# Dilated attention of a hybrid decoder step: the transposes of p of two units in one place, directly behind the values of two others

## The chip, the core and the metric

The kernel runs on one core of a Trainium2 chip. The metric is the device time of one execution in microseconds (us), lower is better. Engines are named as in the profile: PE is TensorE (PEld its weight loads), DVE is VectorE, ACT is ScalarE, POOL is GpSimd, SP issues most DMAs.

## What is computed

One inference step of a one-layer decoder trunk: a Mamba-2 group, a dilated sliding-window attention group and a memory cross-attention group share one input projection and one output projection. The change touches the dilated attention of the prompt (1024 positions, 8 heads of 64). The reference, cut to it:

```python
DILATED_PAIRS = ((128, 1), (512, 4), (2048, 16))
def dilated_prompt(q, k, v):
    for window, dil in DILATED_PAIRS:
...
        sc = jnp.einsum('bnqrhe,bnkrhe->bnrhqk', qb, kb) * scale
        sc = jnp.where(valid[None, :, None, None], sc, -jnp.inf)
        m = jnp.max(sc, axis=-1)
        p = jnp.exp(sc - m[..., None])
        l = jnp.sum(p, axis=-1)
        acc = jnp.einsum('bnrhqk,bnkrhe->bnqrhe', p, vb)
...
        parts.append((back(m), back(l), acc))
    return combine_dilations(parts)
```

`combine_dilations` weighs the three accumulators by their maxima and denominators.

## The kernel before

The dilated attention is done in four passes, `window_attention(hp)` (line 779), one for each pair of heads. A pass begins with transposes of q and k (`qkT`, line 799) and then works through N = 24 units, each one block of 128 queries for both heads: eight of dilation 1, eight of dilation 4, eight of dilation 16. A unit has k = 1 or 2 key blocks of 128.

A unit goes through three stages, each a local function that is called with a step number n:

- `scores(n)` (line 834): four PE matmuls of unit n (`sc`, lines 842 and 843); then for each head DVE masks and takes the maximum (line 847) and ACT takes the exponential with its sum (line 849). The result is the SBUF tile `p`, of which there are 7 buffers.
- `transposed(n)` (line 853): 2k PE transposes of p of unit n-3 into one PSUM bank (`pT`, line 862), and one DVE copy of that bank to SBUF (`pt`, line 863).
- `values(n)` (line 867): only at even n, for the two units n-6 and n-5: the matmuls of pt with v (`o`, line 877; the trace has two records for each). Every fourth unit ends with an ACT copy of the bank (`acc`, line 890).

The order on PE is the order in which the program issues; the other engines' order is set by the scheduler. The step loop sets it:

```python
        for n in range(N + 5):
...
            for work in ((values, transposed), (scores,)):
                ns = sum(w(n) for w in work)
                if ns:
                    yield ns
```

After each yield `drive` (line 150) issues projection matmuls ("fill": tiles `z` and `ga`, lines 336 to 338, in threes) worth 0.6 of the yielded nanoseconds, and `spend` (line 111) moves background work on. The background work of a pass is the `merge` (line 905) of the pass before it. It transposes the maxima and denominators (`mlT`, line 909), goes through DRAM, and then issues eight weight-broadcast matmuls `wb` (line 946), each into a PSUM bank that a DVE product reads (`acc`, line 947). Between two of them lie 900 ns of issued work.

`bank(tag, name)` (line 52) hands out PSUM banks of a tag in turn. `psum_phase("B2", acc=2, sc=2, tp=2, o=2)` gives the tag `tp` two banks, and qkT, mlT, pT and wb all take theirs from it: a request gets the bank of the request before the last, and its writer waits until that one has been read.

Of the kernel before, what the change touches and what calls it, by code (L numbers as in the profile page):

```python
# [11 lines left out]
F32 = mybir.dt.float32  # L12
# [8 lines left out]
P = 128  # L21
# [15 lines left out]
def hybrid_step(ctx: ExitStack, tc: tile.TileContext, i, o):  # L37
# [14 lines left out]
    def bank(tag, name):  # L52
        return phase["pool"].tile([P, 512], F32, tag=tag, name=name, bufs=phase["bufs"][tag])
# [15 lines left out]
    def as32(ap):  # L69
        return ap.bitcast(F32)  # L70
# [21 lines left out]
    def open_pool(name, side="left"):  # L92
        guards[name] = tc.tile_pool(name=name, bufs=1, side=side, reuse_waits="tile")
        return guards[name].__enter__()
# [619 lines left out]
    for f in range(8):  # L714
# [4 lines left out]
        else:  # L719
            if f == 4:  # L720
                until("qc1")
            tp = bank("tp", f"mvT{f}")
# [19 lines left out]
    ap_ = open_pool("apool")  # L742
# [36 lines left out]
    def window_attention(hp):  # L779
# [9 lines left out]
        for c in range(2):  # L789
# [5 lines left out]
            for dst, src in ((q2[0], lambda b: qv[:, b, 0:P]), (kk[0], lambda b: kv[:, b, 0]), (q2[1], lambda b: qv[:, b, P:2 * P]),  # L795
                             (kk[1], lambda b: kv[:, b, 1]), (None, lambda b: lv[:, b])):
                tp = bank("tp", f"qkT_{hp}{c}")
# [24 lines left out]
        units = []  # L822
# [10 lines left out]
        ps, pts, ob, N = {}, {}, None, len(units)  # L833
        def scores(n):
            nonlocal ob
            if n < N:
                pair, u, q, qs_, ks_, vts = units[n]
                w = len(vts) * P
                mask = mask3 if pair == 2 else mask1[:, 256 - w:]
                sc = bank("sc", f"sc_{hp}{n}").rearrange("p (h k) -> p h k", h=2)  # L840
                for h in range(2):
                    PE.matmul(sc[:, h, :w], lhsT=qs_(q[h]), rhs=ks_(kk[h]), start=True, stop=False)  # L842
                    PE.matmul(sc[:, h, :w], lhsT=qs_(q[h]), rhs=ks_(kl[h]), start=False, stop=True)  # L843
                for h in range(2):
                    p = ps[n, h] = ap_.tile([P, 256], F32, tag="p", name=f"p_{hp}{n}{h}", bufs=7)
                    mx, den = ml[:, 0, h, pair, u:u + 1], ml[:, 1, h, pair, u:u + 1]
                    DVE.tensor_tensor_reduce(out=p[:, :w], in0=sc[:, h, :w], in1=mask, scale=-0.125, scalar=HUGE,  # L847
                                             op0=ALU.add, op1=ALU.min, accum_out=mx)
                    ACT.activation(p[:, :w], p[:, :w], AF.Exp, scale=-1.0, bias=mx, accum_out=den)  # L849
                return 4 * max(116.0, w / 2.4 + 12.0)  # L850
            return 0.0

        def transposed(n):
            nonlocal ob
            if 3 <= n < N + 3:
                k = len(units[n - 3][5])
                tp = bank("tp", f"pT_{hp}{n}").rearrange("p (h k) -> p h k", h=2)
                pt = pts[n - 3] = ap_.tile([P, 2, 256], F32, tag="pt", name=f"pt_{hp}{n}", bufs=3)
                for h in range(2):
                    p = ps.pop((n - 3, h))  # L860
                    for t in range(k):
                        PE.transpose(tp[:, h, t * P:(t + 1) * P], p[:, t * P:(t + 1) * P], ident)  # L862
                DVE.tensor_copy(pt[:, :, :k * P], tp[:, :, :k * P])  # L863
                return 218.0 * k
            return 0.0

        def values(n):

# [24 lines left out]
        for n in range(N + 5):  # L893
            if hp < 3 and n in (12, 14):
                load_qk(hp + 1, n // 2 - 6)
            if hp < 3 and n == 18:
                split_qk(hp + 1, 0)
# [5 lines that stand above are left out]
        later(0.0, merge(hp, ml, acc))  # L903

    def merge(hp, ml, acc):


        tp = bank("tp", f"mlT_{hp}")
        PE.transpose(tp[:96, :P], ml.rearrange("p a h r u -> p (a h r u)"), ident)
        mlT = ap_.tile([96, P], F32, tag="mlT", name=f"mlT_{hp}", bufs=1)  # L910
        DVE.tensor_copy(mlT, tp[:96, :P])
        SP.dma_start(ml_d[hp], mlT)
        rb = ap_.tile([16, 2, 3, P], F32, tag="rb", name=f"rb_{hp}", bufs=1)
        for a in range(2):
            src = ml_d[hp, a * 48:(a + 1) * 48].rearrange("(h r u) n -> r h (u n)", h=2, r=3)
            SP.dma_start(rb[:, a, 0], src[0].rearrange("h (t n) -> h t n", t=8))
            for h in range(2):
                SP.dma_start(rb[8 * h:8 * h + 8, a, 1], src[1, h].rearrange("(r t m) -> t r m", r=4, t=8))
                SP.dma_start(rb[8 * h:8 * h + 8, a, 2], src[2, h].rearrange("(r t m) -> t r m", r=8, t=8))
        mm = ap_.tile([16, P], F32, tag="mm", name=f"mm_{hp}", bufs=1)  # L920
        wt = ap_.tile([16, 3, P], F32, tag="wt", name=f"wt_{hp}", bufs=1)

        nat = lambda a, r: rb[:, a, r].rearrange("p (r m) -> p m r", r=(1, 4, 8)[r])
        as_ = lambda t, r: t.rearrange("p (m r) -> p m r", r=(1, 4, 8)[r])
        DVE.tensor_copy(mm, rb[:, 0, 0])
        for r in (1, 2):
            DVE.tensor_tensor(as_(mm, r), as_(mm, r), nat(0, r), op=ALU.min)
        for r in range(3):
            POOL.tensor_tensor(as_(wt[:, r], r), as_(mm, r), nat(0, r), op=ALU.subtract)
        ACT.activation(wt, wt, AF.Exp)  # L930
        for r in range(3):
            POOL.tensor_tensor(nat(1, r), as_(wt[:, r], r), nat(1, r), op=ALU.mult)
        DVE.tensor_copy(mm, rb[:, 1, 0])
        for r in (1, 2):
            POOL.tensor_tensor(as_(mm, r), as_(mm, r), nat(1, r), op=ALU.add)
        DVE.reciprocal(mm, mm)
        POOL.tensor_tensor(wt, wt, mm.unsqueeze(1).to_broadcast([16, 3, P]), op=ALU.mult)
        ACT.copy(wts[:16], wt)
        DVE.tensor_tensor(wts[32:48], wt, as32(wts[:16]), op=ALU.subtract)
        yield 18000.0  # L940
        flat_ = lambda t: t.rearrange("p k n -> p (k n)")
        aacc[hp] = ap_.tile([P, S], F32, tag="att", name=f"att_{hp}")
        out_ = aacc[hp].rearrange("p (t n) -> p t n", n=P)
        for T in range(8):
            wb = bank("tp", f"wb_{hp}{T}")[:, :3 * P]
            PE.matmul(wb, lhsT=selw[:, T], rhs=flat_(wts), start=True, stop=True)
            DVE.tensor_tensor(flat_(acc[:, T]), flat_(acc[:, T]), wb, op=ALU.mult)
            if T % 4 == 3:
                part = slice(T - 3, T + 1)
                POOL.tensor_tensor(acc[:, part, 0], acc[:, part, 0], acc[:, part, 1], op=ALU.add)  # L950
                POOL.tensor_tensor(out_[:, part], acc[:, part, 0], acc[:, part, 2], op=ALU.add)
            yield 900.0
        finished.add(f"att{hp}")
# [636 lines left out]
```

## Time and profile before

| | us |
|---|---|
| median of 3 runs (lowest to highest) | 1181.92 (1181.43 to 1184.21) |
| the profiled execution: its own time | 1178.0 |
| its span, first to last instruction | 1176.2 |
| PE busy | 1106.5 (94% of the span) |
| DVE, ACT, POOL busy | 714.1, 476.5, 395.8 |
| the four attention passes and their fill | about 380 to 638 us of the span |

In the timeline a row is one or more instructions of the same kind that follow each other on an engine. PE is pipelined, so that rows overlap; the cost of a matmul is the distance from its start to the start of the next one. A time in square brackets is idle time of the engine before the row and what ended it.

### The profile page before, as it was taken

What the parts mean: (1) busy time and instruction counts of PE and PEld (TensorE: products, weight loads), DVE (VectorE), ACT (ScalarE), POOL (GpSimd) and SP (SyncE); (2) the same over time, 40 slices, a digit from 0 to 9 for tenths busy, and PEclk for the clock granted to TensorE, in tenths of its full rate; (3) what the DMA queues carried; (4) which work ended last, traced back from release to release, by engine and by line L of the source; (5) the groups of instructions that cost most, each with busy time, mean ns of one, the idle gap of its engine ahead of it and who ended that gap; (6) DMA issues with size and microseconds to landing.
All of it is one profiled execution on the core that took longest, in us unless ns stands there. A gap on an engine that the chain in (4) does not pass through costs nothing.

```text
span 1176.2 us, 19066 instructions
## 1 busy us (share of the span) xinstructions
PE 1106.5 (94%) x7059; PEld 950.5 (81%) x7059; DVE 714.1 (61%) x1524; ACT 476.5 (41%) x1156; POOL 395.8 (34%) x422
## 2 busy tenths in 40 slices
PE   7999999999999999999999999998998898998987
PEld 5867776898888888878888799997998776776865
DVE  5558632358842657566664386877868856265663
ACT  5320110244422666565654133555535654223121
POOL 2355200000134204143322421553534325471761
PEclk9999999999999999999999899999999999998999
DMA  5648547613547422121201321111313423373732
GB/s 205 215 157 269 158 114 209 193 45 113 157 144 201 138 72 82 49 76 55 76 21 40 110 91 52 36 42 49 96 48 102 124 97 103 110 243 110 266 129 74
DMA packets 133149, 137.45 MB, mean 117 GB/s; under 512 B 12440, under 2 KB 98984, under 8 KB 133056
## 3 DMA queue, kind: packets, MB, share of 16 engines
q1 hardware_dynamic: 133056, 136.23, 37.3%
q8 instruction: 56, 0.92, 0.3%
q14 instruction: 37, 0.30, 0.1%
HBM read 106.64 MB, written 29.48 MB: 116 GB/s over the span
## 4 chain that ended last, share of the span: by engine, by line
PE 61%; DMA 12%; DVE 12%; issue 4%; ACT 4%; POOL 4%; SPq 1%; DVEq 0%; POOLq 0%; ACTq 0%
PE conv L336 4%; PE conv L337 4%; PE conv L338 4%; PE pT L862 3%; PE op L1344 3%; PE o L877 3%; PE op L1345 3%; PE op L1347 2%; DMA rsb<-rs_d 2%; PE sc L843 2%; PE sc L842 2%; PE v L233 1%; PE qc L336 1%; PE v L234 1%; PE ga L336 1%
## 5 line engine op out<-in xcount | busy, mean ns | idle before, releaser
L336 PE MATMUL conv<-hTh,wh_conv 128*128 128x348 f32 (+1 forms) x384 | 129.7, 338 | 8.4 <-DVE xc L1086 5.5
L337 PE MATMUL conv<-hTh,wl_conv 128*128 128x348 f32 (+1 forms) x384 | 123.5, 322 | 0.0
L338 PE MATMUL conv<-hTl,wh_conv 128*128 128x348 f32 (+1 forms) x384 | 123.4, 321 | 0.0
L1344 PE MATMUL op<-owh,ofwh 128*128 128x512 f32 x256 | 105.1, 410 | 8.4 <-DVE yo L1354 7.4
L849 ACT ACTIVATE p<-p,ml 128x128 f32<-128x128 f32 (+1 forms) x192 | 84.8, 443 | 62.4 <-DVE ml L847 61.9
L1345 PE MATMUL op<-owl,ofwh 128*128 128x512 f32 x256 | 101.7, 397 | 2.3 <-DVE owl L78 2.3
L1347 PE MATMUL op<-owh,ofwl 128*128 128x512 f32 x256 | 101.6, 397 | 1.0 <-DVE ofwl L78 1.0
L1086 DVE SCALAR_TENSOR_TENSOR xc<-conv,conv_w,xc 128x341 f32<-128x341 f32 (+2 forms) x144 | 81.7, 568 | 31.9 <-ACT xc L1083 29.4
L336 PEld LDWEIGHTS conv<-hTh,wh_conv 128*128 128x128 f32 x384 | 72.6, 189 | 13.6 <-issue 6.9
L847 DVE CUSTOM_DVE_ANT_0 p<-sc,mask 128x128 f32<-128x128 f32 (+1 forms) x192 | 59.3, 347 | 33.5 <-PE sc L843 23.4
L337 PEld LDWEIGHTS conv<-hTh,wl_conv 128*128 128x128 f32 x384 | 72.5, 189 | 1.5
L338 PEld LDWEIGHTS conv<-hTl,wh_conv 128*128 128x128 f32 x384 | 72.5, 189 | 0.0
L863 DVE COPY pt<-pT 128x256 f32<-128x256 f32 (+1 forms) x96 | 52.0, 544 | 32.2 <-PE pT L862 31.6
L336 PE MATMUL z<-hTh,wh_z 128*128 128x344 f32 x192 | 67.0, 349 | 1.7 <-DVE z L372 1.7
L1344 PEld LDWEIGHTS op<-owh,ofwh 128*128 128x128 f32 x256 | 49.0, 192 | 22.5 <-issue 9.5
L1197 POOL TENSOR_TENSOR cx<-cx,xc 128x512 f32<-128x512 f32 x32 | 43.9, 1372 | 62.9 <-ACT cx L1194 62.8
L78 POOL TENSOR_TENSOR wl_conv<-raw_conv,wh_conv 128x1024 fp32r<-128x1024 f32 x16 | 38.7, 2418 | 78.3 <-ACT wh_conv L75 78.3
L337 PE MATMUL z<-hTh,wl_z 128*128 128x344 f32 x192 | 61.7, 321 | 0.0
L338 PE MATMUL z<-hTl,wh_z 128*128 128x344 f32 x192 | 61.6, 321 | 0.0
L1345 PEld LDWEIGHTS op<-owl,ofwh 128*128 128x128 f32 x256 | 49.1, 192 | 12.7 <-DVE owl L78 3.2
L1347 PEld LDWEIGHTS op<-owh,ofwl 128*128 128x128 f32 x256 | 49.0, 191 | 12.0 <-DVE ofwl L78 1.4
L842 PE MATMUL sc<-kk,q 128*128 128x128 f32 (+1 forms) x192 | 55.7, 315 | 0.0
(447 smaller groups left out, 3136.1 us busy)
## 6 DMA issues: line engine op xcount, KB each, us to landing
raw_conv<-w_in SPq DMA_DIRECT2D x16, 512.0 KB
oraw<-w_out SPq DMA_DIRECT2D x16, 512.0 KB
oct<-cat_d SPq DMA_DIRECT2D x16, 512.0 KB
ktw<-cache_win_k SPq DMA_DIRECT2D x24, 256.0 KB
ktw<-cache_win_v SPq DMA_DIRECT2D x24, 256.0 KB
x<-x_prompt SPq DMA_DIRECT2D x8, 512.0 KB
raw_m<-w_mem_kv SPq DMA_DIRECT2D x8, 512.0 KB
ktm<-cache_mem_k SPq DMA_DIRECT2D x16, 256.0 KB
```

What stands on the lines that cost most here:

```text
L336: PE.matmul(ps, lhsT=wh[:, kt], rhs=hTh[:, kt, cs], start=(kt == 0), stop=False)
L337: PE.matmul(ps, lhsT=wl[:, kt], rhs=hTh[:, kt, cs], start=False, stop=False)
L338: PE.matmul(ps, lhsT=wh[:, kt], rhs=hTl[:, kt, cs], start=False, stop=(kt == KT - 1))
L842: PE.matmul(sc[:, h, :w], lhsT=qs_(q[h]), rhs=ks_(kk[h]), start=True, stop=False)
L847: DVE.tensor_tensor_reduce(out=p[:, :w], in0=sc[:, h, :w], in1=mask, scale=-0.125, scalar=HUGE, op0=ALU.add, op1=ALU.min, accum_out=mx)
L849: ACT.activation(p[:, :w], p[:, :w], AF.Exp, scale=-1.0, bias=mx, accum_out=den)
L863: DVE.tensor_copy(pt[:, :, :k * P], tp[:, :, :k * P])
L1086: DVE.scalar_tensor_tensor(xc[:, here.start + cut:here.stop], ps[:, at + cut - 3 + k:at + n - 3 + k], cw[:, ft, k:k + 1], xc[:, here.start ...
L1197: POOL.tensor_tensor(cx, cx, Ct[:, halves[b]], op=ALU.mult)
L1344: PE.matmul(ps[n], lhsT=xh[:, kt], rhs=wh, start=(kt == 0), stop=False)
L1345: PE.matmul(ps[n], lhsT=xh[:, kt], rhs=wl, start=False, stop=(kt == 7 and T == NT))
L1347: PE.matmul(ps[n], lhsT=xl[:, kt], rhs=wh, start=False, stop=(kt == 7))
```

## The change

`transposed` now works at even n only, and then for the two units n-4 and n-3 one after the other. At an even n the PE order is so: values of units n-6 and n-5, transposes of n-4 and n-3, fill, scores of n; at an odd n only scores. The buffers of p go from 7 to 8. To pay for a part of that, the small tile `mm` of `merge` takes the buffer of `mlT`.

```diff
-                    p = ps[n, h] = ap_.tile([P, 256], F32, tag="p", name=f"p_{hp}{n}{h}", bufs=7)
+                    p = ps[n, h] = ap_.tile([P, 256], F32, tag="p", name=f"p_{hp}{n}{h}", bufs=8)
...
         def transposed(n):
-            nonlocal ob
-            if 3 <= n < N + 3:
-                k = len(units[n - 3][5])
-                tp = bank("tp", f"pT_{hp}{n}").rearrange("p (h k) -> p h k", h=2)
-                pt = pts[n - 3] = ap_.tile([P, 2, 256], F32, tag="pt", name=f"pt_{hp}{n}", bufs=3)
+
+            total = 0.0
+            for m in (n - 4, n - 3) if n % 2 == 0 else ():
+                if not 0 <= m < N:
+                    continue
+                k = len(units[m][5])
+                tp = bank("tp", f"pT_{hp}{m}").rearrange("p (h k) -> p h k", h=2)
+                pt = pts[m] = ap_.tile([P, 2, 256], F32, tag="pt", name=f"pt_{hp}{m}", bufs=3)
                 for h in range(2):
-                    p = ps.pop((n - 3, h))
+                    p = ps.pop((m, h))
                     for t in range(k):
                         PE.transpose(tp[:, h, t * P:(t + 1) * P], p[:, t * P:(t + 1) * P], ident)
                 DVE.tensor_copy(pt[:, :, :k * P], tp[:, :, :k * P])
-                return 218.0 * k
-            return 0.0
+                total += 218.0 * k
+            return total
...
-        mm = ap_.tile([16, P], F32, tag="mm", name=f"mm_{hp}", bufs=1)
+        mm = ap_.tile([96, P], F32, tag="mlT", name=f"mm_{hp}", bufs=1)[:16]
```

PE in the second pass, from the second wb of the merge on, before: wb stands behind the scores, then the values of units 0 and 1, the transposes of unit 3, and the third wb.

```order
L946 MATMUL wb_4767<-wts,selw 128x384
L877 MATMUL o_4770<-pt_4703,v_1_4654 64x128 x2
L877 MATMUL o_4770<-pt_4722,v_1_4654 64x128 x4
L862 MATMUL pT_4777<-ident,p_4712 128x128 x2
L862 MATMUL pT_4777<-ident,p_4715 128x128 x2
L946 MATMUL wb_4784<-wts,selw 128x384
```

The same place now:

```order
L880 MATMUL o_4760<-pt_4717,v_1_4654 64x128 x2
L880 MATMUL o_4760<-pt_4722,v_1_4654 64x128 x4
L865 MATMUL pT_4767<-ident,p_4693 128x128 x2
L865 MATMUL pT_4767<-ident,p_4696 128x128 x2
L865 MATMUL pT_4774<-ident,p_4707 128x128 x2
L865 MATMUL pT_4774<-ident,p_4710 128x128 x2
L949 MATMUL wb_4781<-wts,selw 128x384
```

The wb behind the transposes was the second request for a tp bank since the wb before it; now two pT stand directly ahead of it, and it gets the bank of the first of them. The same row of pT, pT and wb stands three times in each of the second, third and fourth pass, at the second, fifth and eighth wb.

PE at the end of the third pass, from the values of unit 19 to the end, before:

```order
L877 MATMUL o_6092<-pt_6098,v_2_5502 64x128 x2
L862 MATMUL pT_6134<-ident,p_6086 128x128
L862 MATMUL pT_6134<-ident,p_6089 128x128
L862 MATMUL pT_6139<-ident,p_6107 128x128
L862 MATMUL pT_6139<-ident,p_6110 128x128
L877 MATMUL o_6144<-pt_6114,v_2_5502 64x128 x2
L877 MATMUL o_6144<-pt_6135,v_2_5502 64x128 x2
L862 MATMUL pT_6149<-ident,p_6123 128x128
L862 MATMUL pT_6149<-ident,p_6126 128x128
L877 MATMUL o_6144<-pt_6140,v_2_5502 64x128 x2
L877 MATMUL o_6144<-pt_6150,v_2_5502 64x128 x2
```

The same place now, from behind the values of unit 19:

```order
L865 MATMUL pT_6129<-ident,p_6060 128x128
L865 MATMUL pT_6129<-ident,p_6063 128x128
L865 MATMUL pT_6134<-ident,p_6071 128x128
L865 MATMUL pT_6134<-ident,p_6074 128x128
L880 MATMUL o_6139<-pt_6130,v_2_5502 64x128 x2
L880 MATMUL o_6139<-pt_6135,v_2_5502 64x128 x2
L865 MATMUL pT_6144<-ident,p_6107 128x128
L865 MATMUL pT_6144<-ident,p_6110 128x128
L865 MATMUL pT_6149<-ident,p_6118 128x128
L865 MATMUL pT_6149<-ident,p_6121 128x128
L880 MATMUL o_6139<-pt_6145,v_2_5502 64x128 x2
L880 MATMUL o_6139<-pt_6150,v_2_5502 64x128 x2
```

Before, the transposes of units 21 and 22 stood ahead of the values of 20 and 21. Now it is those of 20 and 21, the two that the values need, and those of 22 and 23 follow behind the values.

ACT at the end of the same pass, before: the exponentials of unit 22 (6107, 6110), the copy of the values' bank of units 16 to 19, and the exponentials of unit 23 (6123, 6126).

```order
L849 ACTIVATE p_6107,ml_5507<-p_6107,ml_5507 128x128
L849 ACTIVATE p_6110,ml_5507<-p_6110,ml_5507 128x128
L890 COPY acc_5508<-o_6092 128x4x8x16
L849 ACTIVATE p_6123,ml_5507<-p_6123,ml_5507 128x128
L849 ACTIVATE p_6126,ml_5507<-p_6126,ml_5507 128x128
```

Now (unit 22 is 6107 and 6110, unit 23 is 6118 and 6121):

```order
L849 ACTIVATE p_6107,ml_5507<-p_6107,ml_5507 128x128
L893 COPY acc_5508<-o_6087 128x4x8x16
L849 ACTIVATE p_6110,ml_5507<-p_6110,ml_5507 128x128
L849 ACTIVATE p_6118,ml_5507<-p_6118,ml_5507 128x128
L849 ACTIVATE p_6121,ml_5507<-p_6121,ml_5507 128x128
```

Three exponentials stand behind the copy in place of two, in the second, third and fourth pass. In the first pass it is one, before and now.

## Rows read from the trace of the kernel before

**Rows 1.** The page, part 1: PE's busy time, share of the span, instructions.
```profile
PE 1106.5 (94%) x7059; PEld 950.5 (81%) x7059; DVE 714.1 (61%) x1524; ACT 476.5 (41%) x1156; POOL 395.8 (34%) x422
```
**Rows 2.** Busy time by stretch, the four passes: us; engines; granted clock; DMA share, GB/s.
```profile
380.00:638.00 258.00, 249.50 (x2006) 221.43 (x2005) 158.56 (x588) 158.00 (x493) 78.01 (x75) 1.00 0.25 72
```
**Rows 3.** What PE waited for, 380 to 638 us: us in total, times, longest.
```profile
PE pT L862 <- ACT p L849: 1.2, 4, 0.4
PE wb L946 <- DVE acc L947: 1.1, 3, 0.4
```
**Rows 4.** Timeline of PE, first pass: four transposes behind values, four between fill.
```profile
424.50 0.66 PE L862 MATMUL pT<-ident,p 128*128 128x128 f32 x4
424.91 0.40 PE L336 MATMUL z<-hTh,wh_z 128*128 128x344 f32 x1
...
426.41 0.60 PE L862 MATMUL pT<-ident,p 128*128 128x128 f32 x4
426.77 0.40 PE L336 MATMUL z<-hTh,wh_z 128*128 128x344 f32 x1
427.01 0.32 PE L337 MATMUL z<-hTh,wl_z 128*128 128x344 f32 x1
427.17 0.32 PE L338 MATMUL z<-hTl,wh_z 128*128 128x344 f32 x1
```
**Rows 5.** Timeline of PE, first pass: two transposes behind values, two between scores.
```profile
432.57 0.44 PE L862 MATMUL pT<-ident,p 128*128 128x128 f32 x2
432.77 0.35 PE L842 MATMUL sc<-kk,q 128*128 128x128 f32 x1
...
433.29 0.40 PE L862 MATMUL pT<-ident,p 128*128 128x128 f32 x2
433.44 0.35 PE L842 MATMUL sc<-kk,q 128*128 128x128 f32 x1
433.61 0.30 PE L843 MATMUL sc<-kl,q 128*128 128x128 f32 x1
433.73 0.30 PE L842 MATMUL sc<-kk,q 128*128 128x128 f32 x1
```
**Rows 6.** Timeline of PE and DVE, second pass: the third wb.
```profile
462.48 0.55 DVE L947 TENSOR_TENSOR acc<-acc,wb 128x384 f32<-128x384 f32 x1
462.64 0.66 PE L862 MATMUL pT<-ident,p 128*128 128x128 f32 x4
...
463.09 0.45 PE L946 MATMUL wb<-wts,selw 128*128 128x384 f32 x1
...
463.34 0.69 DVE L863 COPY pt<-pT 128x512 f32<-128x512 f32 x1 [0.31 <-PE pT L862]
```
**Rows 7.** Timeline of PE and DVE, second pass: the fifth wb.
```profile
466.26 0.55 DVE L947 TENSOR_TENSOR acc<-acc,wb 128x384 f32<-128x384 f32 x1
...
466.86 0.45 PE L946 MATMUL wb<-wts,selw 128*128 128x384 f32 x1 [0.38 <-DVE acc L947]
```
**Rows 8.** Timeline of PE, DVE and ACT, end of the third pass.
```profile
566.11 0.66 PE L877 MATMUL o<-pt,v 128*64 128x128 f32 x8
...
566.70 0.82 PE L862 MATMUL pT<-ident,p 128*128 128x128 f32 x4
...
567.04 1.09 ACT L890 COPY acc<-o 128x512 f32<-128x512 f32 x1
567.17 0.81 DVE L863 COPY pt<-pT 128x256 f32<-128x256 f32 x2 [0.36 <-PE pT L862]
...
567.92 0.39 ACT L849 ACTIVATE p<-p,ml 128x128 f32<-128x128 f32 x1
...
568.29 0.40 ACT L849 ACTIVATE p<-p,ml 128x128 f32<-128x128 f32 x1
...
569.21 0.42 DVE L863 COPY pt<-pT 128x256 f32<-128x256 f32 x1 [1.23 <-PE pT L862]
570.05 0.53 PE L799 MATMUL qkT<-identr,qs 128*128 128x128 f32 x4
```

## The prediction
> **What bounds the kernel now.** I read the page's engine shares first, then the four attention passes by stretch, then what PE waits for there, then PE's timeline row by row. PE is busy 94% of the span [rows 1] and 249.5 of the 258 us of the attention passes, at a granted clock of 1.00, which is the 2.4 GHz level, while DVE and ACT are each busy about 158 us and POOL 78 [rows 2]. So in the stretch that the change touches PE is the bound: what is issued to PE counts one for one, and work of another engine counts only where PE waits for it. PE waits little: 1.2 us in four places for exponentials ahead of transposes, and 1.1 us in three places for the DVE products ahead of wb [rows 3]. A change of order has some 2 us of waits to win, plus whatever a change between kinds of matmul costs.
>
> **The change, part by part.** It adds and removes no work: the transposes, copies, scores, values and wb are the same in number and shape, and the DMAs and POOL's work keep their order. What moves is PE's order, and with it the order of DVE and ACT.
>
> *A. Fewer, longer blocks of transposes.* Before, a pass has 12 blocks of one unit behind values and 12 that stand alone; the latter join the former, 48 in all. Standing alone between fill, four transposes take 0.36 us from start to the next start (426.41 to 426.77), and the first product behind them is spaced 0.24 where 0.16 is usual, so they cost 0.36 + 0.08 = 0.44 us [rows 4]. Behind values, four take 0.41 (424.50 to 424.91) and two take 0.20 (432.57 to 432.77): two more cost 0.21, so four more cost 0.42 to 0.44 [rows 4, 5]. For two: standing alone between scores they take 0.15, and the next matmul is spaced 0.17 where 0.12 is usual, 0.20 in all, against the 0.21 that they will cost behind values [rows 5]. A transpose costs about 0.105 us in either place, and the way into and out of a block of its own is nearly free. Of the two ends, a saving of the whole 0.08 at each of 48 blocks is 3.8 us, and a loss of 0.02 at each is 1.0 us; the rows sit near zero, so **A = 0**.
>
> *B. wb behind two units.* Two tp banks serve pT and wb in turn. Where wb follows two pT directly, it gets the bank of the first, whose copy DVE has still to do. Before, the wb at 463.09 follows a single pT that began at 462.64, and waited only for a DVE product that ended at 463.03, so the wait ends 0.06 us behind DVE's work. That pT's own copy began 0.70 us after its first transpose and took 0.69 [rows 6]. So a bank of four transposes is free 0.70 + 0.69 + 0.06 = 1.45 us after its first transpose. PE gets there after eight transposes: 0.45 us (462.64 to 463.09) for the first four and 0.44 for the second four, 0.89. The wait is 0.56 us, with nothing else to issue. It comes at 3 wb in each of 3 passes (the fourth pass's merge runs behind the loop): 9 x 0.56 = 5.0 us. Queued behind the waiting wb are fill and the next scores, and DVE and ACT wait for those, but neither is the bound. The 1.1 us of waits for DVE products goes: the fifth wb waited for a product that DVE had behind other work (it ended at 466.81, wb started at 466.86) [rows 3, 7], and that wb now takes a bank of the pair. **B = +3.9**. Bounds: DVE could reach the copy early and leave 0.2 a wb, 1.8 - 1.1 = +0.7, or be late with the scores' maxima and cost 0.8, +7.2 with no wait saved.
>
> A rule bears on this. The Trainium skill, Perfetto Trace Analysis, section Optimizing Tensor Performance, says that independent matmul groups should rotate through different PSUM banks, so that the evacuation of one overlaps the matmuls of the next. It speaks against this change at these nine places, where a pair fills both banks and a third request follows at once: by the rule B stands, without it the sum would be C alone. The 0.06 us between DVE's end and wb's start [rows 6] bears it out.
>
> *C. The end of each pass.* There the fill has run out and nothing covers a wait. In the third pass the end runs from the values of 18 and 19 at 566.11 to the next pass's qkT at 570.05, 3.94 us [rows 8]. Before, the transposes of units 21 and 22 separate the values from the copies that they need. Now, counted from the start of those values: transposes of 20 and 21 at 0.59 (566.11 to 566.70); their two copies start 0.47 later and take 0.81 (567.17), so they end at 1.87; from the start of a last copy to the end of its values it was 0.84 (569.21 to 570.05), 0.42 beyond the copy, so the values end at 2.29. Then the transposes of 22 and 23. ACT's order has three exponentials behind its copy of the values' bank: that copy starts at 0.93 (567.04), the first exponential 0.88 later (567.92) at 1.81, the third 2 x 0.37 later (567.92 to 568.29) at 2.55. From the start of unit 23's last exponential to its pt copy it was 0.92 (568.29 to 569.21), so the copy starts at 3.47 and the pass ends at 4.31: +0.37. Four passes: **C = +1.5**. Bounds: by PE and DVE alone (both copies 0.47 + 0.81 behind 2.29, then 0.42) it ends at 3.99, +0.2 in all; with both waits in full, 0.8 a pass, +3.2. The 1.2 us of waits for exponentials [rows 3] lie in these ends and are in the 3.94.
>
> *The rest at nothing.* The eighth buffer of p removes no wait of PE, since each p is reused only after its transposes. The tile mm shares its buffer with mlT, but it is written from data that came back through DRAM behind mlT's own transfer, so no later wait can come of it. The values' copies come two steps ahead of the values as before, covered by scores and fill of more than 1 us; where that cover is gone is C.
>
> **Sum.** 0 + 3.9 + 1.5 = +5.4 us, from 1178.0 to 1183.4 us for the profiled execution. That one lies 3.9 us under the median of the three runs, 1181.92, so as a median I forecast **1187.3 us**. A measurement of this kernel can tell about 0.3%, 3.5 us, from no change.
>
> **Rivals.**
> - *Bank waits covered.* If DVE's copy is out by the time PE reaches wb, B is about -0.5 to +1 and C alone is left: 1181.92 + 1.5 = 1183.4, no change that can be told. For it: DVE is idle 39% of the span [rows 1]. Against it: the copy cannot start before the unit's last transpose has come through, and 0.70 + 0.69 is longer than 0.89 whatever DVE does. Chance 0.25.
> - *Faster: the way out of a block is what counts.* The place is each join. If eight transposes cost 0.08 less than two times four, each saves the longer first product, 48 x 0.08 = 3.8 us, 1178.1. It decides where four more transposes behind values take under 0.36 us. For it: that first product is 0.24 in place of 0.16 [rows 4]. Against it: the marginal 0.21 for two [rows 5]. It must also not be eaten by B. Chance 0.09.
> - *DVE falls behind.* Two copies in a row (0.69 each [rows 6]) push the maxima of the next scores back, and exponentials and transposes after them. 0.1 us at each of 48 pairs is 4.8 more: 1192.1. Against it: DVE is busy 158 of 258 us [rows 2]. Chance 0.08.
> - That the change does not do what it says is excluded by the order rows.
>
> **How the numbers follow.** The forecast has 0.58. Its part below +3.5 (some 0.06) and the first rival make no change that can be told: 0.31. Slower by more than 0.3% is the rest of the forecast and the third rival: 0.60. Faster is 0.09. The range leaves out the faster rival and the far end of the third: low is the first rival with B at -0.5 and C at its lower bound, about 1181.5; high is A and B as taken with 0.8 us at each of the nine wb and both waits in full at the ends, 5.4 + 2.2 + 1.7, some 9 us above the median: 1191.0.
>
> **What would show it.** Right: in the changed kernel PE waits for pt's copy ahead of wb nine times at about half a us; blocks of eight transposes take about 0.85 us; the end of the third pass takes about 4.3 us. Wrong: no wait of wb for the copy of pt, a block of eight under 0.78 us, or ends no longer than now; and PE waits for exponentials spread over the passes would speak for the third rival.

## The result, and the profile after

The changed kernel took 1188.4 us (median of 5 runs, 1185.73 to 1192.98) against 1181.92 us (median of 5, 1180.54 to 1184.21): a ratio of 1.0057, 95% interval 1.004 to 1.0074. Measured once more later, with 12 runs beside 29 of the kernel before, it took 1183.17 against 1179.97 us: 1.0024, interval 1.0009 to 1.0039. So it is slower, by 0.57% in the first measurement and 0.24% in the second. The forecast was 1187.3 us, slower.

The page, part 1, of the kernel after (span 1187.1 us, own time 1188.9) shows the same number of instructions on PE and DVE as before and nothing that became a bound [rows 1]:

```profile
PE 1109.6 (93%) x7059; PEld 951.7 (80%) x7059; DVE 717.9 (60%) x1524; ACT 475.9 (40%) x1156; POOL 394.8 (33%) x422
```

To compare the attention passes, each window here runs from the first qkT of the first pass to the mlT of the last, so that it holds the same PE instructions in every kernel. Busy time by stretch (columns as in [rows 2]), in turn: before, after, and the second profile of after.

```profile
381.20:634.73 253.53, 245.03 (x1978) 216.97 (x1976) 158.23 (x586) 156.94 (x492) 76.81 (x74) 1.00 0.24 70
```
```profile
382.44:640.46 258.02, 247.63 (x1978) 218.24 (x1975) 157.90 (x586) 155.75 (x492) 76.82 (x74) 0.99 0.24 69
```
```profile
379.95:636.58 256.63, 246.29 (x1978) 216.75 (x1976) 157.81 (x586) 155.64 (x492) 76.80 (x74) 1.00 0.24 69
```

Four passes take 253.5 us before and 256.6 after at a clock of 1.00: **+3.1 us**. The first profile of after has 1.4 us more; its granted clock was 0.50 in one stretch of the second pass, and 3.4 us at half speed can cost up to 1.7. Such a stretch does not need the new order: the kernel of experiment 6 below, in which every engine has the order of the kernel before, has one at the same place, and its passes are 1.4 us longer than before too (254.94 us). In the first profile of after:

```profile
454.40:457.80 3.40, 3.40 (x17) 3.34 (x17) 2.45 (x7) 2.61 (x5) 3.21 (x4) 0.50 0.12 34
```

What PE waited for in the four passes after (us in total, times, longest) answers to [rows 3]:

```profile
PE qkT L799 <- DVE q L808: 5.1, 8, 1.3
PE wb L949 <- DVE pt L866: 1.9, 6, 0.3
PE o L880 <- DVE pt L866: 1.4, 5, 0.3
PE pT L865 <- DVE acc L950: 0.7, 3, 0.3
```

The waits of transposes for exponentials and of wb for products are gone from this list. In their place wb waits for the copies of pt, the values at the ends wait for them too, and three transposes wait for a product. The wait of qkT was 4.9 us before; it plays a part further down.

The timeline of PE and DVE after, second pass, the wb that now follows a pair [rows 6]:

```profile
464.25 1.15 PE L865 MATMUL pT<-ident,p 128*128 128x128 f32 x8
464.95 1.29 DVE L866 COPY pt<-pT 128x512 f32<-128x512 f32 x2 [0.32 <-PE pT L865]
465.69 0.44 PE L949 MATMUL wb<-wts,selw 128*128 128x384 f32 x1 [0.29 <-DVE pt L866]
...
469.82 0.66 PE L865 MATMUL pT<-ident,p 128*128 128x128 f32 x4
470.74 0.63 PE L865 MATMUL pT<-ident,p 128*128 128x128 f32 x4 [0.27 <-DVE acc L950]
471.26 0.44 PE L949 MATMUL wb<-wts,selw 128*128 128x384 f32 x1
```

From the first of eight transposes to wb it is 1.44 us (464.25 to 465.69), as forecast (1.45), where the same block ahead of something else takes 0.85. The copy begins 0.70 us after the first transpose. At all nine places the block takes 1.44 or 1.45 us, +0.59 each. In the middle one of each pass a part of it comes a step earlier: the pair's second unit waits for the product of the wb ahead of the values, and by the time it is through the first bank is nearly free.

### The profile page after: what moved, and what is told of

The parts are those of the page before. It is cut to its first block, busy times and chain, and to the rows that moved or that the text cites. A ratio compares the mean times of both kernels' runs of the same rounds, so it can differ in the third digit from the quotient of the medians.

```text
span 1187.1 us, 19050 instructions
## 1 busy us (share of the span) xinstructions
PE 1109.6 (93%) x7059; PEld 951.7 (80%) x7059; DVE 717.9 (60%) x1524; ACT 475.9 (40%) x1156; POOL 394.8 (33%) x422
## 4 chain that ended last, share of the span: by engine, by line
PE 60%; DVE 13%; DMA 12%; POOL 5%; issue 5%; ACT 4%; SPq 1%; DVEq 0%; POOLq 0%; ACTq 0%
PE conv L336 4%; PE conv L337 4%; PE conv L338 4%; PE o L880 3%; PE pT L865 2%; PE op L1347 2%; PE op L1348 2%; PE sc L842 2%; PE op L1350 2%; PE sc L843 2%; DMA rsb<-rs_d 2%; PE v L233 1%; PE z L336 1%; DVE zt L1237 1%; PE ga L336 1%
## 5 line engine op out<-in xcount | busy, mean ns | idle before, releaser
L866 DVE COPY pt<-pT 128x256 f32<-128x256 f32 (+1 forms) x96 | 48.7, 543 | 34.6 <-PE pT L865 34.1
L843 PE MATMUL sc<-kl,q 128*128 128x128 f32 (+1 forms) x192 | 54.3, 312 | 0.0
```

## The experiments

Each kernel has 12 runs (6 in experiments 8 and 11), taken beside runs of the kernel before, and ratios are to those. "The passes" is the stretch from the first qkT to the last mlT, in one profiled execution. Where a stretch of 3.4 us at half clock stands in it, 1.4 us of it is put down to that, as an estimate from the two profiles of after (258.02 and 256.63).

**1. Another bank for the nine wb, the order unchanged.**

```diff
-            wb = bank("tp", f"wb_{hp}{T}")[:, :3 * P]
+            wb = bank("sc" if T % 3 == 1 else "tp", f"wb_{hp}{T}")[:, :3 * P]
```

> The changed kernel, with the order of every engine as it is; only the second, fifth and eighth wb of a merge, those directly behind a pair of transposes, take a bank of the scores' two in place of a bank of the transposes' two. Bank theory: the wait comes from the bank alone. The nine blocks of eight transposes ahead of such a wb fall from 1.44 to 0.85 us, 9 x 0.59 = 5.3 us less than the changed kernel: about 1183 us, a ratio to the kernel before of about 1.001. Rival (order and clock: long blocks of transposes, or other half-clock stretches, carry the loss whatever the bank): the time stays at the changed kernel's 1188, ratio about 1.0055, even if the wait goes.

Measured: 1182.36 us, ratio 0.9999 (0.9979 to 1.0019). The timeline of PE and DVE at the same place:

```profile
463.28 1.15 PE L865 MATMUL pT<-ident,p 128*128 128x128 f32 x8
463.98 1.29 DVE L866 COPY pt<-pT 128x512 f32<-128x512 f32 x2 [0.32 <-PE pT L865]
464.19 0.42 PE L949 MATMUL wb<-wts,selw 128*128 128x384 f32 x1
```

The copies stand as before, but wb no longer waits for them: 0.91 us in place of 1.44. The nine blocks together fell from 12.97 to 9.05 us, less than the 5.3 expected, because the middle ones still take 1.21 to 1.32: the transposes' wait for the product (0.7 us in three places) stays. The four passes took 253.54 us:

```profile
382.00:635.54 253.54, 244.21 (x1978) 216.52 (x1976) 157.72 (x586) 156.00 (x492) 76.73 (x74) 1.00 0.24 69
```

With the same order on every engine, other banks alone take 3.1 us from the passes (256.63 to 253.54), as much as the change had added. By the blocks it is 3.9; 0.8 of that came back, and qkT waited 6.0 us in this profile in place of 5.0 in the second profile of after. The rival of order and clock falls.

**2. The same wait covered by work instead.** The changed kernel; a flag that `transposed` sets holds wb back until a step of fill or the next scores have been issued.

```diff
                 DVE.tensor_copy(pt[:, :, :k * P], tp[:, :, :k * P])
+                behind[0] = True
...
         for T in range(8):
+            while behind[0]:
+                yield 50.0
```

> The changed kernel, banks as they are, but a wb is held back until one step of fill (three products, 0.48 us) or the next scores stand behind the pair of transposes. Bank theory: the fill covers 0.48 of the 0.59 us, so the nine places cost 9 x 0.1 = 1 us in place of 5.3: about 1184 us, ratio about 1.002; what is left shows as a wait of wb of about 0.1 us behind the fill. Rival (order and clock): ratio about 1.0055 as in the changed kernel.

Measured: 1182.3 us, ratio 1.0007 (0.9987 to 1.0027). Three fill products stand between the pair and wb, and wb comes without a wait:

```profile
466.42 1.14 PE L867 MATMUL pT<-ident,p 128*128 128x128 f32 x8
467.31 0.40 PE L337 MATMUL z<-hTh,wh_z 128*128 128x344 f32 x1
...
467.87 0.42 PE L955 MATMUL wb<-wts,selw 128*128 128x384 f32 x1
```

None of the nine wb shows a wait, not even the 0.1 us that was expected. The passes took 254.91 us with one half-clock stretch, about 253.5 without. So a second, independent remedy also brings the time back.

**3. A dose more of it.** At two of the three places of a pass a second wb follows the first.

```diff
-            yield 900.0
+            if T % 3 != 1 or T == 7:
+                yield 1800.0 if T in (2, 5) else 900.0
```

> The changed kernel with a dose added: at two of the three places of a pass, two wb in place of one stand directly behind the pair (the third wb moves up to the second, the sixth to the fifth), six places in all. Bank theory: the second wb gets the bank of the pair's second unit, and the two copies end 1.29 us after the first began (in the changed kernel's trace 464.95 to 466.24), 0.55 us after the first wb started (465.69): the second starts 0.6 us after the first where 0.17 is usual, +0.44 us at each of six places, 2.6 us more in the passes than the changed kernel, ratio about 1.008. Rival (the wait is a price of leaving the transposes, paid once a block whatever stands behind): no more than the changed kernel, ratio about 1.0055.

Measured: 1189.87 us, ratio 1.0041 (1.0021 to 1.0062). Its passes took 260.57 us, with a stretch at half clock as in the first profile of after (258.02): +2.55, as the bank theory had it. The ratio alone is below the 1.008 expected and can't tell it from the changed kernel; the timeline can:

```profile
465.69 0.44 PE L949 MATMUL wb<-wts,selw 128*128 128x384 f32 x1 [0.29 <-DVE pt L866]
466.17 1.15 DVE L950 TENSOR_TENSOR acc<-acc,wb 128x384 f32<-128x384 f32 x2
466.29 0.44 PE L949 MATMUL wb<-wts,selw 128*128 128x384 f32 x1 [0.16 <-DVE pt L866]
```

The second wb starts 0.60 us after the first (465.69 to 466.29), where 0.17 is usual: the price is paid once for each bank, not once for each block.

**4. Pairs for units 0 to 19 alone, so that the ends stand as before.**

```diff
-            for m in (n - 4, n - 3) if n % 2 == 0 else ():
-                if not 0 <= m < N:
+            for m in (n - 4, n - 3):
+                joined = m < 20
+                if not 0 <= m < N or (n % 2 if joined else m != n - 3):
```

> The changed kernel with pairs for units 0 to 19 alone; units 20 to 23 are transposed one by one as before, so the ends of the four passes stand as before. Bank theory: the ends give back the 0.2 us each that the two traces show (0.9 in all), the nine wb still wait 0.59 us each: about 1187.5 us, ratio about 1.005. Rival (the ends carry the loss, since nothing covers them and they push the next pass): ratio 1.001 or less.

Measured: 1187.45 us, ratio 1.0041 (1.0022 to 1.0059). From the last pass's values of units 18 and 19 to its end it takes 3.84 us, against 4.16 after and 3.93 before, and the nine wb wait as in the changed kernel. But the passes took 256.83 us, no less than the 256.63 of the second profile of after. The four ends are 1.3 us shorter in all, and the step ahead of each is 0.33 us longer, since it now holds the transposes of unit 20 as well (2.43 us from the values of units 16 and 17 to those of 18 and 19, in place of 2.10). So the expected 0.9 us did not come: the ends carry none of the loss that the passes show.

**5. Pairs for units 10 to 19 alone** (the same edit with `joined = 10 <= m < 20`).

> Pairs for units 10 to 19 alone, five blocks a pass and twenty in all; no wb stands behind a pair, and the ends stand as before. Bank theory: joining blocks costs and brings nothing, so 1182 +- 1 us, ratio 1.000 +- 0.001. Rival (long blocks cost in themselves: 6.5 us over 48 joins): 20/48 x 6.5 = +2.7 us, ratio 1.0023. Rival (the way out of a block is a gain that wb and the ends hide): 20 x 0.08 = -1.6 us, ratio 0.9986.

Measured: 1184.23 us, ratio 1.0018 (1.0003 to 1.0033), but the four passes took 253.49 us, as before. By the ratio long blocks seem to cost; by the trace nothing is lost where the pairs stand. The next two runs were made to settle this.

**6. The buffers alone, in the kernel before.**

```diff
-                    p = ps[n, h] = ap_.tile([P, 256], F32, tag="p", name=f"p_{hp}{n}{h}", bufs=7)
+                    p = ps[n, h] = ap_.tile([P, 256], F32, tag="p", name=f"p_{hp}{n}{h}", bufs=8)
...
-        mm = ap_.tile([16, P], F32, tag="mm", name=f"mm_{hp}", bufs=1)
+        mm = ap_.tile([96, P], F32, tag="mlT", name=f"mm_{hp}", bufs=1)[:16]
```

> The kernel before with the change's two edits of buffers alone (eight buffers of p, mm in the buffer of mlT); the order of every engine is that of the kernel before. Every theory: ratio 1.000 +- 0.001, the four passes as long as before. Rival (the buffers' new places or a dependence of mm on mlT cost something, which would also stand behind the 1.0018 of the run with pairs for units 10 to 19): ratio 1.0015 or above.

Measured: 1182.65 us, ratio 0.9996 (0.998 to 1.0013). The passes took 254.94 us with the one half-clock stretch named above, about 253.5 without. The buffers cost nothing that can be told.

**7. Both costs out: experiments 1 and 4 together.**

> Both suspected costs taken out of the changed kernel at once: the nine wb directly behind a pair take a bank of the scores, and units 20 to 23 are transposed one by one, so the ends stand as before. Pairs of units 0 to 19 stay. Bank theory: nothing of the loss is left but the transposes that wait for the DVE product of a wb ahead (0.7 us in the four passes), so within 1 us of the kernel before, ratio 1.000 +- 0.001, and under the run with the wb on the scores' banks alone by up to 0.9 us. Rival (pairs cost in themselves, as the 1.0018 of the run with pairs for units 10 to 19 alone would have it): 40 joins of 48, ratio 1.0035.

Measured: 1180.84 us, ratio 0.997 (0.9953 to 0.9987), better than expected and far from the rival's 1.0035. Its passes took 254.16 us with one half-clock stretch as in the first profile of after, about 252.8 without, 0.8 below the kernel before. So pairs do not cost in themselves, and the 1.0018 of experiment 5 has no place in the passes that explains it; it stays open.

**8. Three banks for the transposes in the kernel before.**

```diff
-    psum_phase("B2", acc=2, sc=2, tp=2, o=2)
+    psum_phase("B2", acc=2, sc=2, tp=3, o=1)
```

> The kernel before, with three PSUM banks for transposes and wb and one for the values in place of two and two. If waits for a bank of the transposes' tag are worth having back: the 1.1 us of wb and a part of the 4.9 us of qkT go, the values' one bank is copied by ACT while scores and fill run, so 2 to 4 us less, ratio 0.997. Rival (the single bank of the values makes the next values wait for ACT's copy, or the waits of qkT are set by the copies' own pace): ratio 1.000 or above.

Measured: 1201.53 us, ratio 1.0152 (1.0122 to 1.0182). What PE waited for in the four passes:

```profile
PE o L877 <- ACT acc L890: 15.6, 8, 4.2
PE wb L946 <- DVE wts L939: 6.4, 3, 2.7
PE sc L842 <- DVE ml L847: 2.0, 2, 1.4
PE z L336 <- DVE z L372: 0.4, 1, 0.4
PE qkT L799 <- DVE q L808: 0.2, 1, 0.2
```

The waits of qkT went as expected (4.9 to 0.2 us), but the values waited 15.6 us for their single bank. Three waits of 4.19 us, one in each pass from the second on, make 12.6 of that, and there ACT itself stood idle:

```profile
479.37 0.58 ACT L890 COPY acc<-o 128x512 f32<-128x512 f32 x1 [2.42 <-POOL att L951]
```

ACT's copy writes `acc`, and POOL is still reading that for the merge of the pass before (it ends at 479.34). In the kernel before, the first two copies of this pass also come only behind POOL (at 477.35 and 478.60, POOL ends at 476.26), but with two banks the values went on meanwhile. The first wb of each merge also came to wait for its weights, 6.4 us. So more banks did help qkT, and the bank was taken from a place where it was needed.

**9. More banks for qkT, taken from the scores,** which are idle at the head of a pass: on the kernel of experiment 7, and on the kernel before.

```diff
-                tp = bank("tp", f"qkT_{hp}{c}")
+                tp = bank("sc" if x % 2 else "tp", f"qkT_{hp}{c}")
```

Here x counts the blocks of qkT (the line of the loop that sets it is left out).

> The kernel with pairs for units 0 to 19 and the nine wb on the scores' banks (0.997 of the kernel before), and beside it the blocks of qkT at the head of a pass take a bank of the transposes and of the scores in turn, four in all in place of two. Bank theory, at another place: PE's 4.9 to 5.6 us of waits of qkT for the copies of q are waits for a bank; they go, as they went with three banks (5.2 us less in qkT), a part comes back where the first scores then wait for the same copies; 3 us less, ratio 0.994 to 0.995. Rival (the copies' own pace sets when scores can begin): all of it comes back, ratio 0.997.

> The kernel before with the same edit of qkT's banks alone. Bank theory: 3 us less, ratio 0.997 to 0.998. Rival (the copies' own pace): 1.000.

Measured: on the pairs 1186.09 us, ratio 1.0041 (1.0017 to 1.0064); on the kernel before 1181.07 us, ratio 1.0008 (0.9992 to 1.0024). Both miss: neither won, and the second is the rival's 1.000. The waits of the first of them:

```profile
PE wb L950 <- DVE wts L943: 7.5, 3, 3.2
PE sc L842 <- DVE ml L847: 1.8, 1, 1.8
```

qkT waits no more, and now PE comes to the first wb of each merge before the weights have been through DRAM and back: one wait was exchanged for another. On the kernel before it is the same: the first wb of each merge waited 5.9 us for the weights, which it did not before. The rival had the right sum and the wrong place: the scores wait once, 1.8 us, and the weights cost the rest. The profiled execution of this kernel was its fastest (1175.15 us, clock 0.990); its twelve runs had a mean granted clock of 0.983, those of the kernel before beside it 0.987. So this profile, 11 us faster than the median, does not show all that the median is made of.

**10. The changed kernel again.**

> The changed kernel as it is, once more, in one call with its two neighbours, for a second profile and a closer ratio. By the passes of the traces (the four passes 2.8 us longer without their half-clock time) the ratio is 1.0025 to 1.004; by the first measurement 1.0057. It tells whether something outside the passes carries a part of the loss.

Measured: 1.0024, as told above. Its passes are the 256.63 us above, and 3.1 us are 0.26%: here the passes carry the whole loss. What the first measurement had beyond that stays open; no profile puts it down to the change. Behind the passes, where the work is the same, its profile has 546.7 us against 541.5 before, but that stretch took 546.4 us in experiment 1, whose ratio was 0.9999, and 543.7 in experiment 6.

**11. The first wb later, the eight closer together,** on the first kernel of experiment 9.

```diff
-        yield 18000.0
+        yield 21500.0
...
-            wb = bank("sc" if T % 3 == 1 else "tp", f"wb_{hp}{T}")[:, :3 * P]
+            wb = bank("sc" if T % 4 == 2 else "tp", f"wb_{hp}{T}")[:, :3 * P]
...
-            yield 900.0
+            yield 450.0
```

> The kernel with pairs for units 0 to 19, with wb and qkT on more banks, and beside that the first wb of a merge 3.5 us of issued work later and the eight closer together (450 in place of 900 ns); the two wb that then stand directly behind a pair take the scores' banks. In the run without this, qkT won its 5.2 us in the passes and the first wb of each merge lost 7.5 us in three places, since it came before the merge's weights were ready. Theory: that wait goes, the four passes shorten by 6 to 7 us, and with it the added half-clock time: ratio to the kernel before 0.992 to 0.995, faster than both kernels. Rival (DVE falls behind: eight products in half the time, and the copies of the pairs between them, so that PE waits there instead): ratio 0.998 to 1.002.

Measured: 1172.43 us against 1182.36, **ratio 0.9911** (0.9886 to 0.9936), faster than both kernels. The four passes:

```profile
382.50:627.73 245.23, 240.89 (x1978) 217.30 (x1976) 159.37 (x586) 156.33 (x492) 76.95 (x74) 1.00 0.26 72
```

and what PE waited for in them:

```profile
PE sc L842 <- DVE ml L847: 1.6, 1, 1.6
PE pT L866 <- ACT p L849: 0.9, 3, 0.4
PE z L336 <- DVE z L372: 0.4, 1, 0.4
PE pT L866 <- DVE acc L951: 0.3, 2, 0.2
PE wb L950 <- DVE wts L943: 0.2, 1, 0.2
```

The wait for the weights fell from 7.5 to 0.2 us, and the passes are 8.3 us shorter than before. Whether the pairs add to this was not tried: the same edits without pairs were not run.

## Why the prediction was right, point by point

**A, switching: forecast 0, about +0.25 us by an estimate.** To see it without waits, each PE matmul of the four passes, without qkT, was given the median distance to the next start of its kind, shape and neighbours over several of the kernels. The sum is 0.2 to 0.4 us longer after than before, by how finely the kinds are told apart. The faster rival's term is there: the first fill product behind transposes takes 0.24 us where 0.16 is usual, and it occurs 26 times in place of 47, which saves 1.8 (0.085 each). But the last transpose of a block is followed by the next start after 0.03 us, and one inside a block after 0.11, so each block end that goes loses the 0.08 again. A way out of a block is free in both orders, as the rows of the prediction had it [rows 4, 5].

**B, wb behind a pair: forecast +5.0 - 1.1 = +3.9, measured +5.3 - 2.2 = +3.1.** The nine places, the bank, the 1.44 us and the wait in each were as forecast; 0.59 us each makes 5.3. The term that was mis-sized is what goes: it was taken from the waits, 1.1 us [rows 3]. The timeline of PE before, at the fifth wb, shows that the wait costs more than its idle time:

```profile
466.21 0.28 PE L843 MATMUL sc<-kl,q 128*128 128x256 f32 x1
466.86 0.45 PE L946 MATMUL wb<-wts,selw 128*128 128x384 f32 x1 [0.38 <-DVE acc L947]
```

From start to start it is 0.65 us, where 0.12 is usual behind such a score: 0.53 lost, in place of the 0.38 idle, because the last matmul's run is counted as busy. Three such places are 1.6 us, and the blocks of transposes ahead of the second wb, 0.54, 0.67 and 0.47 us where 0.41 is usual, are 0.45 more; the third wb's add 0.1. What went was twice the forecast; even so B carries the loss. That the transposes of the pair's second unit would wait for DVE's product at the middle wb was not foreseen; it changed where the wait shows, not its sum.

The rule that the prediction drew on (the Trainium skill, Perfetto Trace Analysis, section Optimizing Tensor Performance: matmul groups should rotate through PSUM banks) is borne out by experiment 1, where nothing but the bank was changed, and by experiment 3.

**C, the ends: forecast +1.5; +0.9 in the ends, and about nothing in the passes.** From the start of the values of units 18 and 19 the four ends took 3.90, 4.45, 4.15 and 4.16 us after, against 3.66, 4.27, 3.94 and 3.93 before. The third, after (PE, DVE and ACT, as [rows 8]):

```profile
569.88 0.66 PE L880 MATMUL o<-pt,v 128*64 128x128 f32 x8
...
570.47 0.66 PE L865 MATMUL pT<-ident,p 128*128 128x128 f32 x4
...
570.66 1.07 ACT L893 COPY acc<-o 128x512 f32<-128x512 f32 x1
...
570.94 0.76 DVE L866 COPY pt<-pT 128x256 f32<-128x256 f32 x2
571.42 0.77 PE L880 MATMUL o<-pt,v 128*64 128x128 f32 x8 [0.30 <-DVE pt L866]
571.52 0.38 ACT L849 ACTIVATE p<-p,ml 128x128 f32<-128x128 f32 x1
...
572.12 1.02 PE L865 MATMUL pT<-ident,p 128*128 128x128 f32 x4
...
572.28 0.39 ACT L849 ACTIVATE p<-p,ml 128x128 f32<-128x128 f32 x1
...
573.18 0.42 DVE L866 COPY pt<-pT 128x256 f32<-128x256 f32 x1 [0.16 <-PE pT L865]
574.03 0.36 PE L799 MATMUL qkT<-identr,qs 128*128 128x128 f32 x2
```

Step by step the chain is the one forecast: transposes at 0.59, copies 0.47 later, the values done at 2.24 (forecast 2.29), where the next transposes start, the third exponential, 0.90 to the last copy, 0.85 to the end. One number differs: ACT's copy of the values' bank began 0.78 us after the start in place of 0.93, because one exponential less stands ahead of it. That 0.15 is the whole distance between 4.31 and 4.15. The other ends added 0.24, 0.18 and 0.23 us, where the third's 0.37 had been carried over to all four.

But a longer end is not a longer pass, and this step of the prediction failed. Counted from the values of units 18 and 19, an end now holds eight transposes where it held six, as the order rows of the change show: those of unit 20 stood ahead of that point before. Two transposes behind values take 0.20 us [rows 5], and 4 x 0.20 is nearly all of the 0.9. What the end gains, the rest of the pass gives up, to within 0.1 us. The first pass shows it, since no wb stands in it: up to the values of units 18 and 19 it took 54.94 us before and 54.80 in the second profile of after, its end 3.66 and 3.90, the whole 58.60 and 58.70. Experiment 4 says the same from the other side: shorter ends, passes no shorter. The prediction put moved transposes at nothing in A and then counted them as a cost in C.

**The sum.** 0.25 + 3.1 + 0 = 3.3 us against 3.1 measured in the passes. The forecast of +5.4 us lies within the first interval (+4.7 to +8.7 us) and above the second (+1.1 to +4.6). So the mechanism of B was right and its size nearly so, and that the first median of 1188.4 us came within about 1 us of the forecast is luck: C was too large by 1.5, B by 0.8, and the first measurement held some 3 us that the change does not explain.

**The rivals.** Bank waits covered: all nine places waited. DVE falling behind: no transposes outside the ends waited for exponentials. The way out of a block: its 1.8 us are there, and the block ends that go take them back.

## What to carry to other kernels

When work that rotates through few banks is bunched, look for the next request behind the bunch: it gets the oldest bank of the bunch, and the cost is (first write to free) minus (time PE spends in the bunch), once for each bank asked for. The remedy is a bank of a tag that is idle there, or one step of other work in between. When a wait is removed, read the distance from start to start rather than the idle time, and ask what PE will now reach too early: here 5 us of qkT waits came back as 7.5 us of waits for the merge's weights until wb was moved back as well. When a stretch is compared before and after, count whether it still holds the same instructions: the ends here looked 0.2 us longer each because one unit's transposes had moved into them.

## What the runs showed of the hardware that was not expected

Long waits of PE often stood beside stretches at the lower of the clock's two levels, but not always. In the kernel of experiment 8 a wb started at 535.71 after 2.73 us of waiting, and the granted clock was 0.50 (1.2 GHz) from 535.0 on for 6.8 us, then back near 1.00. Busy time by stretch; PE was busy 7.25 of the 10 us before:

```profile
525.00:535.00 10.00, 7.25 (x52) 6.31 (x50) 8.76 (x28) 8.45 (x27) 6.07 (x9) 1.00 0.19 54
535.00:541.80 6.80, 6.09 (x29) 5.46 (x30) 3.18 (x9) 1.09 (x4) 0.00 (x0) 0.50 0.00 0
541.80:545.00 3.20, 3.20 (x25) 3.09 (x23) 2.29 (x9) 2.39 (x6) 0.97 (x1) 0.99 0.00 0
```

Its six runs had a mean granted clock of 0.979, the kernel before beside it 0.985. With a span of about 1200 us, that 0.006 is at most some 7 us of the 17 to 18 us it lost, by estimate. Each of its three waits of 4.19 us has such a stretch beside it too. But in the profile of the first kernel of experiment 9, PE waited 3.20 us for the wb at 527.25, and the clock stayed at 1.00 through its passes; and the stretch of 3.4 us in the second pass stands in the profiles of after and of experiments 2, 3, 6 and 7, where no wait is that long. So that the waits cause the stretches is not shown. The nine short waits of the changed kernel did not lower its mean clock: it was 0.987 in its twelve later runs, as the kernel before had.
